# Which engine's queue issues the mixer's stores: SyncE's or ScalarE's

## The chip, the cores and the metric

The kernel runs on one core of a Trainium2 chip. The metric is the device time of one execution in microseconds, lower is better. An execution's time is a little longer than its span, the time from the first to the last instruction in the trace. TensorE (PE) does the matrix products, VectorE (DVE), ScalarE (ACT) and GpSimd (POOL) the element-wise work. SyncE (SP) computes nothing here and only issues DMAs. An engine runs its instructions in order, and when one of them waits for a semaphore, everything behind it on that engine waits too; this holds for the instruction that issues a DMA as for any other.

## What is computed

One layer of a hybrid encoder on 17 chunks of 128 tokens: chunk 0 holds 8 running streams of 16 new frames, chunks 1 to 16 hold one new stream of 2048 frames. All arithmetic is in f32.

```python
proj = jnp.einsum('bld,de->ble', x, w_in)              # 1024 -> u, v, z (1024 each), xbc 1536, dt 16
y_g  = gelu(u) * (W_s @ layer_norm(gelu(v)) + b_s)     # gMLP: a causal 128x128 product per head and chunk
xbc  = silu(causal_conv(xbc))                          # four taps over time
y    = ssd_scan(x, softplus(dt + bias), a, B, C, h0)   # Mamba-2: products inside a chunk, a state between chunks
y_s  = gated_rms_norm(y + d_skip * x, z, g)
x    = layer_norm(ALPHA * x + concat([y_g, y_s]) @ w_out)
x    = layer_norm(ALPHA * x + (relu(x @ w_ff1) ** 2) @ w_ff2)
```

## The kernel before, in words

**Phases.** The mixer (projection, convolution, scan, gMLP) runs until about 1066 us of the span; then come the product with w_out and the first norm, and after them the two products of the feed-forward part, which the change doesn't touch. An f32 product is made of three passes over split operands: `split` (L55, L56) casts a tile on ACT to its high part and subtracts on DVE for the low part.

**Blocks and units.** The mixer goes over the chunks in three blocks of 6, 6 and 5. In each block 18 units run in the order z0, x4, x5, x0, x1, z1, x2, x3, z2, z3, u0 to u3, v0 to v3. A unit multiplies the block's tokens by 256 columns of w_in. One group of 24 matmuls (8 slices of the contraction in 3 passes) fills one of four PSUM tiles (pool psA): of 128x384 in `fl_matmul` (L231) for x and u, of 128x256 in `tl_matmul` (L239) for z and v. Elementwise work empties the tile: for u and v `gelu2`, whose four steps alternate between ACT and DVE (L245 ACT, L246 DVE, L247 ACT, L248 DVE) and which reads PSUM until its last step; for z one ACT step (L275) and one on DVE (L276); for x two ACT steps (L301, L302), the convolution on DVE (L308), L313 on ACT and a product on DVE. PE may thus be ahead of that work by the tiles that are free, and no further.

**What goes through DRAM.** In block 0 the weights of a unit are loaded from w_in (L133), split, and both parts are kept in DRAM by L127 (2 MB a unit, 18 times); blocks 1 and 2 load them back by L117. The units' outputs go to DRAM too: u by L257, v by L266, z by L279, B and C by L328, x by L330 and by L334 (four DMAs of 32 partitions a unit). Between the units stand tasks: the scan of a chunk and group (`ssd`), which loads x, bt, bc, e and z (L418 to L427), and ends with a square on ACT (L505), a small root on POOL and a product on DVE (L507), stored by L508; and the gMLP of a chunk (`gmlp`), which loads v and u (L523, L525), multiplies on PE (L537) and then on POOL (L546), and stores by L547. The gMLP tasks of a block run in the first third of the next one, those of block 2 beside the product with w_out, whose weights are loaded by L631 and scaled by L636 (ACT) and L637 (DVE).

**The order.** The kernel is written in program order; a scheduler in the build sets the order on each engine, and the semaphores follow from it. Every DMA is issued by SP, and its landing counts on one of eight landing semaphores, taken in turn by all DMAs of the program: before a DMA is issued, its engine also waits for the landing of the one that took the same semaphore before.

```python
def gelu2(out, ps, n):
    t = ap.tile([P, 384], F32, name="gt", tag="gt", bufs=3)
    nc.scalar.activation(t[:, :n], ps, AF.Square)
    nc.vector.scalar_tensor_tensor(t[:, :n], t[:, :n], 1.0 / GC, ps, op0=ALU.add, op1=ALU.mult)
    nc.scalar.activation(t[:, :n], t[:, :n], AF.Tanh, scale=GK * GC)
    nc.vector.scalar_tensor_tensor(out, t[:, :n], 1.0, ps, op0=ALU.add, op1=ALU.mult)
```

The functions that the change touches, and what calls them:

Of the kernel before, what the change touches and what calls it, by code (L numbers as in the profile page):

```python
# [7 lines left out]
F32 = mybir.dt.float32  # L8
# [6 lines left out]
P = 128  # L15
# [75 lines left out]
def mixer_heads(ctx, tc, right, psA, A, O, dr, small, sp, ident, select, rsqrt, split, yg_d, ys_d):  # L91
    nc = tc.nc
# [31 lines left out]
    def keep_parts(u, w):  # L124
        n = 272 if u == "z0" else 256
        parts[u] = dr.tile([P, 2, KD, n], F32, name=f"w_{u}")
        nc.sync.dma_start(parts[u], w[:, :, :, :n].bitcast(F32))  # L127

    def load_w_half(w, u, q):
        n = 272 if u == "z0" else 256  # L130
# [119 lines left out]
    def unit_u(b, w, q):  # L250
        c0, n = BLOCKS[b]
        uo = ap.tile([P, 2, 6 * P], F32, name="uo", tag="ao")
        for f in range(2):
            for o, m in halves(n):
                ps = fl_matmul(w, f, o, m)
                gelu2(uo[:, f, o:o + m], ps[:, :m], m)
        nc.sync.dma_start(state[b]["u"][:, 2 * q:2 * q + 2, :], uo[:, :, :n * P])  # L257

    def unit_v(b, w, q):
        c0, n = BLOCKS[b]  # L260
        vo = ap.tile([P, 6, 256], F32, name="vo", tag="ao")
        for j in range(n):
            ps = tl_matmul(w, j, 256)
            gelu2(vo[:, j], ps[:, :256], 256)
            nc.vector.bn_stats(state[b]["vst"][:, j, q], vo[:, j])
        nc.sync.dma_start(state[b]["v"][:, :, q * 256:(q + 1) * 256].rearrange("c p f -> p c f"), vo[:, :n])  # L266

    def unit_z(b, w, q):
        c0, n = BLOCKS[b]
        nn = 272 if q == 0 else 256  # L270
        zo = ap.tile([P, 6, 256], F32, name="zo", tag="ao")
        for j in range(n):
            ps = tl_matmul(w, j, nn)
            t = ap.tile([P, 384], F32, name="zt", tag="gt", bufs=3)
            nc.scalar.activation(t[:, :256], ps[:, :256], AF.Tanh, scale=0.5)  # L275
            nc.vector.scalar_tensor_tensor(zo[:, j], t[:, :256], 1.0, ps[:, :256], op0=ALU.add, op1=ALU.mult)  # L276
            if q == 0:
                nc.vector.tensor_add(state[b]["dt"][:, j], ps[:, 256:272], dtb)
        nc.sync.dma_start(state[b]["z"][:, :, q * 256:(q + 1) * 256].rearrange("c p f -> p c f"), zo[:, :n])  # L279

    def unit_x(b, w, q):
        c0, n = BLOCKS[b]
        nd = 1 if c0 == 0 else 0
        npr = (n - nd) * P
        fl_out = ap.tile([P, 2, 6 * P], F32, name="fo", tag="ao") if q >= 4 else None
        tl_out = ap.tile([P, 6, 256], F32, name="to", tag="ao") if q < 5 else None
        for f in range(2):
            ft = 2 * q + f
            raw = ap.tile([P, 3 + 6 * P], F32, name="raw", tag="raw", bufs=1)
            acc = ap.tile([P, 6 * P], F32, name="acc", tag="acc")  # L290
            nc.gpsimd.tensor_copy(raw[:, :3], carry[:, ft])
            if nd:
                rawd = ap.tile([P, NS, 3 + DS], F32, name="rawd", tag="rawd", bufs=1)
                nc.gpsimd.tensor_copy(rawd[:, :, :3], cst_in[:, ft])
            for o, m in halves(n):
                ps = fl_matmul(w, f, o, m)
                s = 0
                if nd and o == 0:
                    s = P
                    nc.scalar.copy(rawd[:, :, 3:], ps[:, :P].rearrange("p (s t) -> p s t", s=NS))  # L300
                nc.scalar.copy(raw[:, 3 + o + s - nd * P:3 + o + m - nd * P], ps[:, s:m])  # L301
                nc.scalar.activation(acc[:, o:o + m], ps[:, :m], AF.Identity, bias=cb[:, ft:ft + 1], scale=cw[:, ft, 3:4])  # L302
            for k in range(3):
                if nd:
                    ad = acc[:, :P].rearrange("p (s t) -> p s t", s=NS)
                    nc.vector.scalar_tensor_tensor(ad, rawd[:, :, k:k + DS], cw[:, ft, k:k + 1], ad, op0=ALU.mult, op1=ALU.add)
                aa = acc[:, nd * P:n * P]
                nc.vector.scalar_tensor_tensor(aa, raw[:, k:k + npr], cw[:, ft, k:k + 1], aa, op0=ALU.mult, op1=ALU.add)  # L308
            nc.gpsimd.tensor_copy(carry[:, ft], raw[:, npr:npr + 3])
            if nd:  # L310
                nc.gpsimd.tensor_copy(cst_out[:, ft], rawd[:, :, DS:])
            t = ap.tile([P, 6 * P], F32, name="ct", tag="ct", bufs=1)
            nc.scalar.activation(t[:, :n * P], acc[:, :n * P], AF.Tanh)  # L313
            dst = fl_out[:, f, :n * P] if q >= 4 else acc[:, :n * P]
            nc.vector.scalar_tensor_tensor(dst, t[:, :n * P], 1.0, acc[:, :n * P], op0=ALU.add, op1=ALU.mult)
            if q < 4:

                nc.vector.transpose(tl_out.rearrange("p c (k f) -> p (c k) f", f=64)[:, :4 * n, 32 * f:32 * f + 32],
                                    dst.rearrange("p (k i) -> p k i", i=32))
            if q == 4:  # L320
                for j0 in range(0, n, 3):
                    m = min(3, n - j0)
                    pt = psB.tile([P, 4, P], F32, name="pt", tag="b")
                    for j in range(m):
                        nc.tensor.transpose(pt[:, j], dst[:, (j0 + j) * P:(j0 + j + 1) * P], ident)
                    nc.scalar.copy(tl_out[:, j0:j0 + m, f * P:(f + 1) * P], pt[:, :m])
        if q >= 4:
            nc.sync.dma_start(state[b]["bc"][:, :, q - 4, :], fl_out[:, :, :n * P])  # L328
        if q == 4:
            nc.sync.dma_start(state[b]["xs"][:, :, q * 256:(q + 1) * 256].rearrange("c p f -> p c f"), tl_out[:, :n])  # L330
        if q < 4:
            xs = state[b]["xs"].rearrange("c (m i) f -> i (c m) f", i=32)
            for c in range(4):
                nc.sync.dma_start(xs[:, :, q * 256 + c * 64:q * 256 + c * 64 + 64],  # L334
                                  tl_out[32 * c:32 * c + 32, :n].rearrange("p c (k f) -> p (c k) f", f=64))


# [71 lines left out]
    def ssd(b, j, g):  # L409
# [95 lines left out]
        nc.scalar.activation(t, y, AF.Square, accum_out=ss)  # L505
        rsqrt(ss, ss, 1.0 / 512, 4 * EPS)
        nc.vector.tensor_scalar(y, y, ss, None, op0=ALU.mult)  # L507
        nc.sync.dma_start(ys_d[c0 + j][:, g * 512:(g + 1) * 512], y)  # L508


    def gmlp(b, j):
# [7 lines left out]
        for q in range(2):  # L519
            hq = slice(4 * q, 4 * q + 4)  # L520
            fq = slice(512 * q, 512 * q + 512)
            v = half("v")
            nc.sync.dma_start(v, s["v"][j, :, fq])  # L523
            u = half("ug").rearrange("p (k t) -> p k t", k=4)
            nc.sync.dma_start(u, s["u"][:, hq, j * P:(j + 1) * P])  # L525
            nc.vector.tensor_scalar(v, v, mv[:, 0:1], rs, op0=ALU.subtract, op1=ALU.mult)
            wm = wt[:, hq]
            if dec:
                wm = half("wt8").rearrange("p (k t) -> p k t", k=4)
                nc.vector.memset(wm, 0.0)  # L530
                for r in range(NS):
                    nc.sync.dma_start(wm[r * DS:(r + 1) * DS, :, r * DS:(r + 1) * DS], A["gmlp_wsT"][:DS, hq, :DS])
                select(wm, [[0, 4], [1, P]], 0, -1)
            ps = psB.tile([P, 4, P], F32, name="sg", tag="b")
            o = fp.tile([P, 4, P], F32, name="og", tag="og", bufs=2)
            for i in range(4):
                nc.tensor.matmul(ps[:, i], v[:, i * P:(i + 1) * P], wm[:, i], start=True, stop=True)  # L537
            for i in range(4):
                h = 4 * q + i
                if dec:  # L540
                    k = cst[:, h, :DS].unsqueeze(1).to_broadcast([P, NS, DS])
                    i0, oo = ps[:, i].rearrange("p (s t) -> p s t", s=NS), o[:, i].rearrange("p (s t) -> p s t", s=NS)
                else:
                    k, i0, oo = cst[:, h], ps[:, i], o[:, i]
                nc.vector.scalar_tensor_tensor(oo, i0, lgh[:, h:h + 1], k, op0=ALU.mult, op1=ALU.add)
            nc.gpsimd.tensor_mul(u, u, o)  # L546
            nc.sync.dma_start(yg_d[c0 + j][:, hq, :], u)  # L547
            if dec:
                for i, nm in enumerate(("gmlp_ln_g", "gmlp_ln_b")):
                    k = half("lk")  # L550
                    nc.sync.dma_start(k, row(nm)[:, fq].to_broadcast([P, 512]))
                    (nc.vector.tensor_mul, nc.vector.tensor_add)[i](v, v, k)
                nc.sync.dma_start(O["v_sample"][:, fq], v)
# [608 lines left out]
```

## Time and profile before

| | us |
|---|---|
| median of 3 runs | 2829.03 (2822.79 to 2832.81) |
| the profiled execution | 2822.72 |
| its span | 2821.0 |
| PE busy | 2753.9 (98%) |
| DVE busy | 1816.1 (64%) |
| ACT busy | 1096.0 (39%) |
| POOL busy | 395.1 (14%) |

The profiled execution is 6.3 us, 0.2%, under the median. Busy times leave out the issuing of DMAs and all waiting. In the rows further down an instruction that issues a DMA has the engine's name with a q (SPq), `out<-in` are tile names, `x3` is how many instructions a row joins, and `[1.93 <-DVE vo L248]` says that the engine stood idle for 1.93 us ahead of it until DVE's instruction at L248 on tile vo had ended. Idle time of PE is what counts where it is 98% busy; idle time of the others counts only where it ends in one of PE's.

### The profile page before, as it was taken

The numbers are of one execution on the slowest core, as the hardware profiler recorded it, in microseconds if no ns is written. First come the engines' busy times: TensorE is split into PE (matmuls) and PEld (weight loads), VectorE is DVE, ScalarE is ACT, GpSimd is POOL, SyncE is SP. The second block draws the span as 40 slices with busy tenths as digits, with TensorE's granted clock in tenths as the row PEclk, the third lists the DMA queues.
The fourth block names the chain that finished last, engine by engine and source line by source line (L and its number), as shares of the span: only waits on it lengthen the run. The fifth ranks groups of instructions, "written<-read, shape, count | busy, mean of one in ns | idle before, by whom it ended". The sixth has DMA issues, their size and how long they took to land.

```text
span 2821.0 us, 42133 instructions
## 1 busy us (share of the span) xinstructions
PE 2753.9 (98%) x15814; PEld 2525.6 (90%) x15814; DVE 1816.1 (64%) x2836; ACT 1096.0 (39%) x2024; POOL 395.1 (14%) x547
## 2 busy tenths in 40 slices
PE   9999999999999998999989999999999999999998
PEld 8988899999999997887879999999999888888886
DVE  6766667645585457665558667667775356644887
ACT  5445423323333333100115556556665323333343
POOL 2214223323233312000100000000000000000022
PEclk9999999999999999999999999999999999999999
DMA  9897888766697768888579858667877468855764
GB/s 316 257 297 250 281 288 272 228 221 217 218 305 220 244 218 302 279 260 273 159 217 342 292 214 286 222 223 259 276 233 259 152 233 300 299 173 190 272 206 171
DMA packets 492316, 699.83 MB, mean 248 GB/s; under 512 B 74560, under 2 KB 379088, under 8 KB 485584
## 3 DMA queue, kind: packets, MB, share of 16 engines
q1 hardware_dynamic: 492112, 697.14, 74.8%
q8 instruction: 124, 2.03, 0.3%
q14 instruction: 80, 0.66, 0.1%
HBM read 474.04 MB, written 223.00 MB: 247 GB/s over the span
## 4 chain that ended last, share of the span: by engine, by line
PE 77%; DMA 12%; DVE 6%; issue 1%; ACT 1%; POOL 1%; SPq 1%; DVEq 0%; ACTq 0%; POOLq 0%
PE pf L858 22%; PE pf L1075 22%; PE psfl L231 13%; PE pstl L239 10%; PE po L683 4%; PE yd L446 2%; DMA w1p<-in_w_ff 2%; DMA w1s<-w1p 2%; PE pf L1040 2%; DMA v<-v 1%; DMA xv<-xtt 1%; PE st L483 1%; DMA v<-vo 1%; DMA e<-at 1%; PE yo L489 1%
## 5 line engine op out<-in xcount | busy, mean ns | idle before, releaser
L858 PE MATMUL pf<-xt,w 128*128 128x384 f32 (+1 forms) x4032 | 671.8, 329 | 14.6 <-ACT w L55 11.4
L858 PEld LDWEIGHTS pf<-xt,w 128*128 128x128 f32 x4032 | 669.2, 189 | 17.4 <-ACT w L55 12.3
L1075 PE MATMUL pf<-w,ht 128*128 128x512 f32 x2688 | 618.2, 389 | 0.0
L1075 PEld LDWEIGHTS pf<-w,ht 128*128 128x128 f32 x2688 | 504.6, 188 | 104.6
L231 PE MATMUL psfl<-xw,w 128*128 128x384 f32 (+1 forms) x2880 | 494.9, 330 | 0.0
L231 PEld LDWEIGHTS psfl<-xw,w 128*128 128x128 f32 x2880 | 475.5, 188 | 9.0 <-issue 8.6
L239 PE MATMUL pstl<-w,xw 128*128 128x256 f32 (+1 forms) x3264 | 411.0, 286 | 8.4 <-ACT w L55 6.5
L239 PEld LDWEIGHTS pstl<-w,xw 128*128 128x128 f32 x3264 | 396.4, 190 | 21.0 <-issue 11.8
L683 PE MATMUL po<-wout,mx 128*128 128x512 f32 x1632 | 379.5, 394 | 12.0 <-ACT mx L55 8.1
L683 PEld LDWEIGHTS po<-wout,mx 128*128 128x128 f32 x1632 | 309.2, 190 | 79.1 <-ACT mx L55 8.8
L56 DVE TENSOR_TENSOR ht<-hr,ht 128x1536 fp32r<-128x1536 f32 (+1 forms) x84 | 132.3, 1577 | 128.0 <-ACT ht L55 126.5
L76 POOL TENSOR_SCALAR frs<-fmv 128x1 f32<-128x1 f32 x17 | 8.9, 524 | 1291.6 <-DVE fmv L996 1291.0
L55 ACT CAST ht<-hr 128x1536 fp32r<-128x1536 f32 (+1 forms) x84 | 112.2, 1337 | 194.7 <-PE pf L1075 142.0
L56 DVE TENSOR_TENSOR w<-w1s,w 128x512 fp32r<-128x512 f32 x192 | 132.0, 691 | 41.0 <-ACT w L55 36.0
L55 ACT CAST w<-w1s 128x512 fp32r<-128x512 f32 x192 | 118.3, 619 | 64.1 <-PE pf L858 57.0
L308 DVE SCALAR_TENSOR_TENSOR acc<-raw,cw,acc 128x640 f32<-128x640 f32 (+1 forms) x108 | 111.4, 1031 | 14.1 <-ACT acc L302 12.7
L56 DVE TENSOR_TENSOR w<-w2r,w 128x512 fp32r<-128x512 f32 x144 | 93.8, 686 | 36.8 <-ACT w L55 36.6
L55 ACT CAST w<-w2r 128x512 fp32r<-128x512 f32 x144 | 83.3, 618 | 87.3 <-PE pf L1075 56.9
L438 ACT ACTIVATE e<-e,nacum 128x128 f32<-128x128 f32 x272 | 83.6, 389 | 66.8 <-POOL e L69 66.7
L55 ACT CAST w<-w1r 128x512 fp32r<-128x512 f32 x96 | 59.4, 618 | 98.6 <-PE pf L858 95.3
L247 ACT ACTIVATE gt<-gt 128x256 f32<-128x256 f32 (+1 forms) x116 | 52.3, 451 | 95.9 <-DVE gt L246 95.9
L849 ACT ACTIVATE hc<-hc 128x384 f32<-128x384 f32 (+3 forms) x144 | 87.1, 608 | 1.8
(214 smaller groups left out, 2875.4 us busy)
## 6 DMA issues: line engine op xcount, KB each, us to landing
w1s<-w1s SPq DMA_DIRECT2D x48, 1024.0 KB, 6.7
hr<-hv SPq DMA_DIRECT2D x56, 768.0 KB, 6.1
w2r<-in_w_ff SPq DMA_DIRECT2D x112, 256.0 KB, 5.6
w<-w_x SPq DMA_DIRECT2D x12, 2048.0 KB, 10.5
w1r<-in_w_ff SPq DMA_DIRECT2D x48, 512.0 KB, 6.7
hv<-hs SPq DMA_DIRECT2D x32, 768.0 KB, 5.2
ws<-in_w_in SPq DMA_DIRECT2D x34, 512.0 KB, 7.7
e<-at SPq DMA_DIRECT2D x34, 512.0 KB, 6.7
```

What stands on the lines that cost most here:

```text
L55: nc.scalar.copy(hi, src)
L56: nc.vector.tensor_sub(lo, src, hi.bitcast(F32))
L231: nc.tensor.matmul(ps[:, :n], w[:, a, k, f * P:(f + 1) * P], xw[:, b, k, o:o + n], start=(q, i, k) == KORDER[0], stop=(q, i, k) == KORDER[-1])
L239: nc.tensor.matmul(ps[:, :n], xw[:, a, k, j * P:(j + 1) * P], w[:, b, k, :n], start=(q, i, k) == KORDER[0], stop=(q, i, k) == KORDER[-1])
L308: nc.vector.scalar_tensor_tensor(aa, raw[:, k:k + npr], cw[:, ft, k:k + 1], aa, op0=ALU.mult, op1=ALU.add)
L438: nc.scalar.activation(e[:, h], e[:, h], AF.Exp, bias=s["nacum"][:, i:i + 1])
L446: nc.tensor.matmul(yd[:, h * HD:(h + 1) * HD], e[:, h], xdt[:, h * HD:(h + 1) * HD], start=True, stop=True)
L683: nc.tensor.matmul(acc[c][d], m[c][k // 4][:, a, k % 4], W[q][:, w, i, d * 512:(d + 1) * 512], start=k == 0 and (a, w) == (0, 0), stop=k = ...
L849: nc.scalar.activation(t, t, AF.Square)
L858: nc.tensor.matmul(o, W[i][:, u, k], X[i][:, v, k, :n], start=q + k == 0 and not more, stop=q == 2 and k == 3, skip_group_check=True)
L1040: nc.tensor.matmul(ps[d], h[:, u, k, f], w[d][:, v], start=k + f + q == 0, stop=(k, f, q) == (n - 1, 1, 2))
L1075: nc.tensor.matmul(acc[l], h[:, u, m, j * P:(j + 1) * P], w[m][:, v], start=kg + q + m == 0, stop=(kg, q, m) == (3, 2, 3))
```

## The change

All nine stores that the mixer's units and tasks make are issued from ACT instead of SP; the loads and a few stores of results (L480, L494, L553, the convolution's carry) stay on SP. That is 179 DMAs: L127 18, L257 12, L266 12, L279 12, L328 6, L330 3, L334 48, L508 34, L547 34. SP's program goes from 1279 rows to 1115, ACT's from 1613 to 1770. From the second group of the product with w_out on, the order of both programs is the same.

```diff
@@ -124,7 +124,7 @@
-        nc.sync.dma_start(parts[u], w[:, :, :, :n].bitcast(F32))
+        nc.scalar.dma_start(parts[u], w[:, :, :, :n].bitcast(F32))
@@ -254,7 +254,7 @@
-        nc.sync.dma_start(state[b]["u"][:, 2 * q:2 * q + 2, :], uo[:, :, :n * P])
+        nc.scalar.dma_start(state[b]["u"][:, 2 * q:2 * q + 2, :], uo[:, :, :n * P])
@@ -263,7 +263,7 @@
-        nc.sync.dma_start(state[b]["v"][:, :, q * 256:(q + 1) * 256].rearrange("c p f -> p c f"), vo[:, :n])
+        nc.scalar.dma_start(state[b]["v"][:, :, q * 256:(q + 1) * 256].rearrange("c p f -> p c f"), vo[:, :n])
@@ -276,7 +276,7 @@
-        nc.sync.dma_start(state[b]["z"][:, :, q * 256:(q + 1) * 256].rearrange("c p f -> p c f"), zo[:, :n])
+        nc.scalar.dma_start(state[b]["z"][:, :, q * 256:(q + 1) * 256].rearrange("c p f -> p c f"), zo[:, :n])
@@ -325,13 +325,13 @@
-            nc.sync.dma_start(state[b]["bc"][:, :, q - 4, :], fl_out[:, :, :n * P])
+            nc.scalar.dma_start(state[b]["bc"][:, :, q - 4, :], fl_out[:, :, :n * P])
-            nc.sync.dma_start(state[b]["xs"][:, :, q * 256:(q + 1) * 256].rearrange("c p f -> p c f"), tl_out[:, :n])
+            nc.scalar.dma_start(state[b]["xs"][:, :, q * 256:(q + 1) * 256].rearrange("c p f -> p c f"), tl_out[:, :n])
-                nc.sync.dma_start(xs[:, :, q * 256 + c * 64:q * 256 + c * 64 + 64],
+                nc.scalar.dma_start(xs[:, :, q * 256 + c * 64:q * 256 + c * 64 + 64],
@@ -505,7 +505,7 @@
-        nc.sync.dma_start(ys_d[c0 + j][:, g * 512:(g + 1) * 512], y)
+        nc.scalar.dma_start(ys_d[c0 + j][:, g * 512:(g + 1) * 512], y)
@@ -544,7 +544,7 @@
-            nc.sync.dma_start(yg_d[c0 + j][:, hq, :], u)
+            nc.scalar.dma_start(yg_d[c0 + j][:, hq, :], u)

```

The scheduler places each store in ACT's order. Three places follow. In the first, the end of block 0's unit v2 (the tiles `w_v_3834` and `v_264` in DRAM are the kept weights of v3 and the block's v), SP had this before:

```order
L418 DMA xs<-xs_266 128x512
L127 DMA w_v_3834<-w 2048x1x256
L266 DMA v_264<-vo 128x6x256
L139 DMA xs_in<-in_xT 128x1024
L508 DMA ys_97<-xs 128x512
```

and ACT has this in the changed program:

```order
L438 ACTIVATE e<-e,nacum_272 128x128 x8
L127 DMA w_v_3834<-w 2048x1x256
L266 DMA v_264<-vo 128x6x256
L247 ACTIVATE gt<-gt 128x256
L245 ACTIVATE gt<-pstl 128x256
```

The store of the kept weights and behind it that of a finished v unit now stand between two steps of ACT's own work, ahead of the gelu steps of the next chunk.

The second place is ACT in the x units of block 1, where the gMLP tasks of block 0 run (`raw`, `acc` and `ct` are the convolution's tiles, `ug` the gMLP's result). Before:

```order
L313 ACTIVATE ct<-acc 128x768
L301 COPY raw<-psfl 128x384
L302 ACTIVATE acc<-psfl,cb,cw 128x384
L301 COPY raw<-psfl 128x384
L302 ACTIVATE acc<-psfl,cb,cw 128x384
L313 ACTIVATE ct<-acc 128x768
```

and in the changed program:

```order
L313 ACTIVATE ct<-acc 128x768
L301 COPY raw<-psfl 128x384
L302 ACTIVATE acc<-psfl,cb,cw 128x384
L301 COPY raw<-psfl 128x384
L302 ACTIVATE acc<-psfl,cb,cw 128x384
L547 DMA yg_80<-ug 128x512 x2
L313 ACTIVATE ct<-acc 128x768
```

Two stores of the gMLP's result, each of which waits for POOL's product, now stand ahead of L313.

The third place is ACT beside the first group of the product with w_out. Before, eight steps of L636 follow one another:

```order
L55 CAST mx<-myt 128x512 x2
L55 CAST wout<-wos 128x1024 x2
L55 CAST mx<-myt 128x512 x2
L636 ACTIVATE wout<-wos,ng 128x1024 x8
L55 CAST mx<-mxs 128x512 x2
```

and in the changed program:

```order
L547 DMA yg_90<-ug 128x512 x2
L636 ACTIVATE wout<-wos,ng 128x1024 x2
L547 DMA yg_91<-ug 128x512
L636 ACTIVATE wout<-wos,ng 128x1024
L547 DMA yg_91<-ug 128x512
L547 DMA yg_92<-ug 128x512
L636 ACTIVATE wout<-wos,ng 128x1024
L547 DMA yg_92<-ug 128x512
L636 ACTIVATE wout<-wos,ng 128x1024 x2
```

The stores of the last chunks' gMLP results now stand among the steps of L636.

## Rows read from the trace of the kernel before

**Rows 1.** The page's first part: busy time, share of the span, instructions.
```profile
PE 2753.9 (98%) x15814; PEld 2525.6 (90%) x15814; DVE 1816.1 (64%) x2836; ACT 1096.0 (39%) x2024; POOL 395.1 (14%) x547
```
**Rows 2.** Windows: stretch, length, busy us per engine, PEclk, DMA share, GB/s.
```profile
0.00:383.00 383.00, 368.48 (x2420) 347.58 (x2420) 257.09 (x431) 172.76 (x371) 108.89 (x194) 1.00 0.87 282
...
420.00:757.00 337.00, 334.63 (x2300) 322.60 (x2299) 204.39 (x343) 115.78 (x286) 106.82 (x128) 1.00 0.71 229
...
1065.00:1128.00 63.00, 53.81 (x257) 43.54 (x256) 49.76 (x91) 19.36 (x25) 19.95 (x18) 0.95 0.95 322
```
**Rows 3.** Waits of PE, 0 to 1128 us: total us, times, longest.
```profile
PE sg L537 <- DVE v L526: 5.2, 3, 3.3
PE yo L475 <- DMA h<-in_state_ssm: 3.8, 3, 2.2
...
PE pc L429 <- DMA bc<-bc: 2.2, 2, 1.2
...
PE pstl L239 <- DVE vo L248: 1.9, 1, 1.9
PE yd L446 <- POOL xdt L441: 1.8, 1, 1.8
```
**Rows 4.** PE's timeline: start, length us, what, count (one row of two stretches).
```profile
372.05 10.99 PE L239 MATMUL pstl<-w,xw 128*128 128x256 f32 x88
...
452.74 16.97 PE L231 MATMUL psfl<-xw,w 128*128 128x384 f32 x96
```
**Rows 5.** Waits of SP's queue, 0 to 1128 us: total us, times, longest.
```profile
SPq L508 <- DVE xs L507: 86.7, 20, 8.2
SPq L418 <- DMA ys<-xs: 57.1, 28, 4.8
```
**Rows 6.** Instructions of L508, L334, L279: ns of one issue, min/median/max.
```profile
L508 SPq DMA_DIRECT2D ys<-xs x34: 319/320/1357, 198.9 to 1031.3; - x34
...
L334 SPq DMA_DIRECT2D xs<-to x48: 318/747/3372, 94.5 to 904.3; - x48
...
L279 SPq DMA_DIRECT2D z<-zo x12: 371/1268/3622, 30.7 to 932.5; - x12
```
**Rows 7.** SP's timeline at the end of block 0 (v1 to v3).
```profile
326.89 3.12 SPq L266 DMA_DIRECT2D v<-vo  x1
...
353.38 0.53 SPq L127 DMA_DIRECT2D w_v<-w  x1
354.00 3.60 SPq L266 DMA_DIRECT2D v<-vo  x1
...
372.82 10.25 SPq L139 DMA_DIRECT2D xs_in<-in_xT  x2
```
**Rows 8.** ACT's timeline at the end of block 0.
```profile
357.64 0.42 ACT L247 ACTIVATE gt<-gt 128x256 f32<-128x256 f32 x1 [3.02 <-DVE gt L246]
...
383.08 0.42 ACT L247 ACTIVATE gt<-gt 128x256 f32<-128x256 f32 x1 [5.11 <-DVE gt L246]
```
**Rows 9.** Timelines of ACT and POOL in block 1's x units.
```profile
462.91 0.85 ACT L313 ACTIVATE ct<-acc 128x768 f32<-128x768 f32 x1 [8.74 <-DVE acc L308]
...
480.03 0.85 ACT L313 ACTIVATE ct<-acc 128x768 f32<-128x768 f32 x1 [6.58 <-DVE acc L308]
...
460.01 1.99 POOL L546 TENSOR_TENSOR ug<-ug,og 128x512 f32<-128x512 f32 x1 [2.52 <-DVE og L545]
...
475.22 3.90 POOL L546 TENSOR_TENSOR ug<-ug,og 128x512 f32<-128x512 f32 x2 [1.74 <-DVE og L545]
```
**Rows 10.** Timelines of POOL, ACT and PE beside the first w_out group.
```profile
1120.92 1.44 POOL L546 TENSOR_TENSOR ug<-ug,og 128x512 f32<-128x512 f32 x1 [4.20 <-DVE og L545]
1123.83 2.20 POOL L546 TENSOR_TENSOR ug<-ug,og 128x512 f32<-128x512 f32 x1 [1.46 <-DMA wos<-in_w_out]
...
1122.26 1.15 ACT L636 ACTIVATE wout<-wos,ng 128x1024 fp32r<-128x1024 f32 x1 [1.53 <-DMA wos<-in_w_out]
...
1124.94 5.32 PE L683 MATMUL po<-wout,mx 128*128 128x512 f32 x22 [1.55 <-DVE wout L637]
```

## The prediction, made before the changed kernel was run

> **What bounds the kernel now.** I read the busy times first: PE is busy for 98% of the span, ACT for 39% [rows 1]. Next come the windows, because the change touches only the mixer and the first product with w_out, which fill the first 1128 us; there PE is busy for 368.48 of 383 us in block 0 and for 334.63 of 337 us in the x, z, u and v units of block 1, and only 53.81 of 63 us at the start of the w_out product [rows 2]. So nothing that the change does to ACT or SP counts until PE waits for it. Then I read what PE waits for [rows 3]. Four of its waits end with data that a load brought: sg behind the scaled v 5.2, h 3.8, bc 2.2 and xdt (the loaded xs times dt) 1.8 us, 13.0 us together. A quicker queue of loads can give back this much and hardly more. One other wait matters below: 1.9 us for DVE's last gelu step (vo), at the border of blocks 0 and 1. SP itself waits a lot, 86.7 us at L508 for DVE alone [rows 5], but SP computes nothing; its waits cost only what arrives in the 13.0 us.
>
> Last I measured how far ACT may fall behind before PE notices. PE needs 10.99 us for 88 matmuls of 128x256, so 24 x 10.99 / 88 = 3.0 us for a group that fills one PSUM tile, and 24 x 16.97 / 96 = 4.2 us for one of 128x384 [rows 4]. There are four tiles. With one being emptied, three are cover: about 9.0 us in z and v units, 12.7 us in x and u units, provided that ACT and DVE were not already behind.
>
> **Part by part: what leaves SP.** 179 issues and their waits leave it, 86.7 us of waits at L508 being the largest entry. The loads behind them can go out earlier, but not all do: L418 waits 57.1 us for the landing of ys<-xs [rows 5], that is, its tile comes free only when the store has landed, and which engine issued the store changes nothing in that. Bounds of the gain: nothing, and the whole 13.0 us. I take a quarter, 3.3 us, since the largest wait of a load names a landed store and not a held queue.
>
> **What ACT gets as work.** No row shows a DMA issued by ACT in this kernel. The nearest rows are SP's: 0.320 us the median at L508, 0.747 at L334, 1.268 at L279 [rows 6]. For these 94 issues that is 34 x 0.320 + 48 x 0.747 + 12 x 1.268 = 62 us; the other 85 at 0.32 to 1.27 us are 27 to 108 us. So ACT gets 89 to 170 us in the first 1128 us, at the least nothing if it issues for free, and never a gain. That is up to 15% more of its time, on top of 45% in block 0 (172.76 of 383) and 34% in block 1 (115.78 of 337) [rows 2]. Spread in pieces of about 1 us under a cover of 9.0 to 12.7 us, it costs nothing. If the cover is gone (ACT and DVE already behind), each piece counts in full.
>
> **What ACT gets as waits.** A store waits for the last producer of its tile (DVE's L507, L248, L276; POOL's L546), for a landing semaphore, and for room in the queue. Behind the waiting store stand ACT's next gelu, tanh or cast steps; for these wait DVE, then the PSUM tile, then PE.
>
> - Steady units. The order in ACT puts L508 one or a few steps behind L505, and two small POOL steps and L507 lie between. I count 1 to 2 us a time, an estimate from lengths of steps like these; well inside 9.0 us. Cost 0.
> - Block 1's x units. Two stores of ug stand ahead of L313. POOL's products end at 460.01 + 1.99 = 462.00 and 475.22 + 3.90 = 479.12 us; L313 itself starts only at 462.91 and 480.03, having waited 8.74 and 6.58 us for DVE [rows 9]. The new wait lies inside the old one: cost 0. The work that covers it is DVE's convolution; were DVE earlier, up to the 3.90 us of the POOL pair would show.
> - End of block 0. Behind the 2 MB store of kept weights the next issue takes long: L266 took 3.12 us at 326.89, and 3.60 us at 354.00, right after L127 at 353.38 [rows 7]. In the changed order both stand on ACT, ahead of the next gelu steps. ACT is not early there: it waits for DVE between two steps of one gelu, 3.02 us at 357.64 [rows 8]. So the cover is thin, and part of the hold lies in that wait. Between nothing and 3.12 + 3.60 = 6.7 us I take half, 3.4 us.
> - Border of blocks 0 and 1. L266 of unit v2 stands near the loads of x for block 1. The pair of loads behind it held SP for 10.25 us [rows 7], because of tiles and landings not yet free. If that store holds ACT as long, 10.25 us meet a cover of 9.0 us, of which nothing is left at the border: ACT already waits 5.11 us for DVE at 383.08 [rows 8], and PE 1.9 us for DVE's step [rows 3]. Bounds: nothing (the hold lies inside the 5.11 us and more), and 10.25. I take 2.0 us, near the wait that PE has there now.
> - Start of the w_out product. Of the last stores, one stands ahead of the sixth L636 and one ahead of the seventh. The seventh started at 1122.26; POOL's last product ends at 1123.83 + 2.20 = 1126.03 [rows 10], so it would start 3.8 us later. PE waits here for DVE's step behind it (1.55 us at 1124.94 [rows 10]), so no cover is left. In the other direction, the loads of w_out and v no longer stand behind L547 on SP, which brings L636 and POOL's chain forward. Bounds: nothing and 3.8; I take half, 1.9 us.
>
> **The sum.** 3.4 + 2.0 + 1.9 - 3.3 = +4.0 us. Against the profiled execution, 2822.72 + 4.0 = 2826.7 us. That execution lies 6.3 us under the median of 2829.03, and the price adds to either, so the median becomes 2833.0 us. About 0.3%, 8.5 us, is what a measurement of this kernel can tell from no change: the forecast is inside it.
>
> **Rivals.**
>
> A, faster: the loads come early. If every wait of PE that a load ends goes, and ACT's holds stay covered everywhere, the time is 2829.0 - 13.0 = 2816.0 us. For it: SP waits 86.7 us at L508 with loads queued behind. Against it: L418's 57.1 us name the landing of a store [rows 5], the DMA engines are 71 to 87% busy in blocks 0 and 1 and 95% at the w_out product [rows 2], and 5.2 of the 13.0 us lie at the gMLP's v, which a store must write first. The Trainium skill, page "Perfetto Trace Analysis", section on DMA optimizations, advises what this change does: one engine for input DMAs and another for output DMAs. By that advice the time would be A's.
>
> B, slower: ACT is held for longer than the PSUM tiles cover. Its place is the end of block 0, units v1 to v3 and the border, and the same hold at the sixth and seventh L636. It decides from the point where a hold is longer than three groups, 9.0 us, or where ACT enters it already behind. Its price is 3.12 + 3.60 + 10.25 + 3.8 = 20.8 us, hence 2849.8 us. For it: ACT is at 45% in block 0, in which the 18 stores of 2 MB fall, and it waits for DVE already. Against it: each hold would have to reach PE whole.
>
> C, no change: the two queues stay coupled. The eight landing semaphores are shared by all DMAs, so a load on SP may still wait for the landing of a store on ACT and a store for a load's, and PE's waits stay where they are: 2829.0 us. Apart from that, the Trainium skill, page "DMA: Bandwidth & Descriptors", section "Issuing engines are not separate DMA queues", says that DMAs of all issuers run on the same 16 engines and that a second issuer saves only the time of issuing. By this the loads would gain little, which is C's side; the 3.12 and 3.60 us of issuing behind a full store [rows 7] show that here the saved part is not always small.
>
> **How the numbers follow.** Chances: the forecast 0.45, A 0.15, B 0.27, C 0.13. The forecast's own range is 2822 to 2841 us (its terms at a half up or down). Low end of the range: A's 2816. High end: B's 2849.8 plus the 3.90 us of the block 1 units, were their cover gone, about 2854. Some 0.07 lies below and 0.11 above. Faster by over 0.3% (below 2820.5) is most of A: 0.13. Slower by over 0.3% (above 2837.5) is B and the upper end of the forecast, 0.27 + 0.07 = 0.34. Within 0.3%: C, the rest of the forecast and of A, 0.53.
>
> **What would show it.** In the profile after: SP's waits at L508 are gone, and L418's for ys<-xs have stayed. PE's waits for load-ended tiles go from 13.0 to about 10 us; if they fall to 3 or less and nothing comes in, A is right. At the end of block 0 ACT issues L266 with 3 us or more behind L127, and PE's waits for vo grow from 1.9 to some 7 us; if they grow by 15 or more, B is right. Beside the w_out product ACT's L636 is held until POOL's L546 ends, and PE's wait for wout grows by about 2 us. L313 in block 1 starts no later against the PE groups than before. The forecast is wrong if ACT's issues take much longer than 0.3 to 1.3 us each, since then the steady units pay too, or if the order of PE's tasks, which the scheduler also moved, lets PE wait in a place where it did not wait before.

## The result

The changed kernel is slower: 2843.84 us in the median of 13 runs (2834.71 to 2851.01) against 2824.44 us for the kernel before in the same sessions. The ratio, estimated from all runs and not from the two medians (whose quotient is 1.0069), is 1.0058, with a 95% interval of 1.0046 to 1.0071, or +16 us on the 2829.03 us that the prediction started from. That is inside the range of 2816 to 2854 us, but only because the range reaches to rival B's price: it is above the forecast's own 2822 to 2841 us, four times the forecast of +4.0 us, and nearer to rival B (+20.8 us). Rivals A (faster) and C (no change) did not come.

The changed kernel's profiled execution took 2834.71 us, the lowest of its 13; its span is 2833.0 us, 12.0 us more than before. So the traces below show 12 of the some 16 us. The first lines are from the page of the changed kernel: busy times, then DMA queues (q10 is ACT's).

```profile
PE 2759.2 (97%) x15814; PEld 2527.8 (89%) x15814; DVE 1811.8 (64%) x2836; ACT 1093.0 (39%) x2024; POOL 396.7 (14%) x547
...
q1 hardware_dynamic: 387616, 599.09, 63.9%
q10 hardware_dynamic: 104496, 98.05, 10.0%
```

The change does what it says: 98 MB go through a second queue. PE runs the same 15814 matmuls and is busy for 5.3 us longer than in [rows 1] (2759.2 - 2753.9); the other 6.7 of the 12.0 us are idle time. The mean granted clock of the two profiled executions is the same, 0.991, but it falls to 0.50 in other places. Up to the second group of the w_out product it stands at 0.50 for 27 us in all in the changed kernel and for 14 us in the kernel before, which costs PE some 7 us more; behind that it is the other way round, 17 against 27 us. In the changed kernel a stall of PE began ahead of each fall.

Next, what PE waits for in the changed kernel, 0 to 1140 us: total us, times, longest.

```profile
PE yd L446 <- DVE e L439: 7.8, 7, 2.1
...
PE yd L446 <- POOL xdt L441: 5.9, 5, 1.9
PE sg L537 <- DVE v L526: 4.7, 2, 3.7
PE yo L475 <- DMA h<-in_state_ssm: 2.7, 2, 2.1
PE po L683 <- DVE wout L637: 2.5, 2, 1.6
...
PE psfl L231 <- DVE zo L276: 1.6, 1, 1.6
PE po L683 <- ACT wout L636: 1.5, 1, 1.5
```

The four load-ended waits of [rows 3], 13.0 us, are now xdt 5.9, v 4.7, h 2.7 and bc 0: 13.3 us. Nothing was gained there. What grew are the waits of the scan's product yd, for e (after DVE) and xdt (after a load of xs). The wait for vo is gone. SP's queue (same view) shows what became of its waits:

```profile
SPq L418 <- DMA ys<-xs: 196.2, 25, 12.3
```

The waits of [rows 5] at L508 (86.7 us) left SP and came back at the load of xs, which needs the landing of the same store: 57.1 us have become 196.2.

**Where the time goes.** I took the start of the first matmul of each unit in both traces; the table gives how much later the changed kernel is (us), over five stretches. The last column is the second half of the first w_out group, from its 97th matmul to the second group's first. Unit names are those of the order of units, with the block ahead: 0x5-0x0 is from the start of x5 to that of x0 in block 0. "Rest 1, 2" is what else blocks 1 and 2 lose until the w_out product.

```
kernel (which stores ACT issues)   0x5-0x0  0x0-1z0  1z1-1z2  rest 1, 2  w_out 1st-2nd group   ratio
changed (all nine)                   3.7      8.7      8.0      -5.9          3.3              1.0058
all but L127                         0.0     15.3      7.9      -4.4          5.1              1.0039
all but L508                         3.5     17.3      8.7       0.5          5.0              1.0076
all but L334                         3.6      6.7      0.3       0.9          4.9              1.0011
all but L547                         2.9     13.7      7.1      -5.4          0.4              1.0050
all but L127, L334                   0.0      8.7      0.0       4.8          4.1              1.0014
only L127                            0.0      5.2      0.0       6.7          1.8              1.0018
only L334                            0.0      9.5      0.0       1.4          0.8              1.0030
only L508                            0.0      2.4      0.0       1.8          2.0              0.9993
only L508, L547                      0.0     -2.4      0.0       1.0          1.4              0.9996
none, four more copies on ACT        0.0     -0.1      0.0      -1.0          2.5              0.9992
L127 on POOL                         0.0     -1.1      0.0       4.5          0.3              0.9975
all nine on POOL                     0.0     -2.1      1.5       8.7          2.2              1.0040
```

The first and third columns are sharp: a loss is there or it is not. The second is spread, since the scheduler also places the scans anew in most of these kernels. The ratios come from several runs, the columns from one execution each, and one execution can stray: behind the columns, from the second w_out group on, where the change touches nothing, these traces differ from the one before by -5.9 to +8.3 us.

### The profile page after: what moved, and what is told of

Read it like the earlier page. It is cut to its first block, busy times and chain, and to the rows that moved or that the text cites. A ratio compares the mean times of both kernels' runs of the same rounds, so it can differ in the third digit from the quotient of the medians.

```text
span 2833.0 us, 42155 instructions
## 1 busy us (share of the span) xinstructions
PE 2759.2 (97%) x15814; PEld 2527.8 (89%) x15814; DVE 1811.8 (64%) x2836; ACT 1093.0 (39%) x2024; POOL 396.7 (14%) x547
## 4 chain that ended last, share of the span: by engine, by line
PE 68%; DMA 15%; DVE 9%; ACT 3%; issue 2%; ACTq 1%; POOL 1%; SPq 1%; DVEq 0%; POOLq 0%
PE pf L1075 22%; PE pf L858 22%; PE psfl L231 8%; PE pstl L239 8%; PE po L683 3%; DMA w1p<-in_w_ff 2%; PE yd L446 2%; DMA w1s<-w1p 2%; PE pf L1040 2%; DMA e<-at 1%; DVE acc L308 1%; DVE w L56 1%; PE st L483 1%; ACTq L334 1%; DMA xs<-to 1%
## 5 line engine op out<-in xcount | busy, mean ns | idle before, releaser
L858 PE MATMUL pf<-xt,w 128*128 128x384 f32 (+1 forms) x4032 | 669.8, 328 | 14.9 <-ACT w L55 12.0
L231 PEld LDWEIGHTS psfl<-xw,w 128*128 128x128 f32 x2880 | 476.8, 188 | 12.8 <-issue 10.2
L55 ACT CAST mx<-mxs 128x512 fp32r<-128x512 f32 x34 | 20.1, 620 | 162.9 <-DMA mxs<-yg 98.4
```

The lines of the kernel that those rows point to most:

```text
L55: nc.scalar.copy(hi, src)
L231: nc.tensor.matmul(ps[:, :n], w[:, a, k, f * P:(f + 1) * P], xw[:, b, k, o:o + n], start=(q, i, k) == KORDER[0], stop=(q, i, k) == KORDER[-1])
L858: nc.tensor.matmul(o, W[i][:, u, k], X[i][:, v, k, :n], start=q + k == 0 and not more, stop=q == 2 and k == 3, skip_group_check=True)
```

## The experiments

Theory H: ACT, held while it issues or waits for a store, makes DVE's steps and the scans late. Theory D: the stores of ys land later, and so do the loads that wait for them. Theory O: only the order that the scheduler made of it is worse.

**L127 back on SP.**

```diff
+        nc.sync.dma_start(parts[u], w[:, :, :, :n].bitcast(F32))      # L127, the rest as changed
```

> The changed kernel with L127, the 2 MB stores of the kept weights, back on SP. In the changed kernel (1.0058 of before, about +16 us) the stores behind L127 held ACT for 3.56 (L328), 6.23 and 4.56 us (L266). Theory H (ACT is held while it issues a store behind a full one, and DVE's steps for gelu and scan come late): these three fall below 1 us each, block 0 gives back most of its 12 us, and the ratio to before is 1.001 to 1.003. Theory D (the stores of ys wait in ACT's order, land later, and the scans' loads of xs with them): L127 is no part of it, the ratio stays at 1.004 to 1.006. Theory O (the scheduler put PE's tasks in a worse order, the queues matter little): anything, the ratio follows the order and no single hold.

Measured: 1.0039 (1.0022 to 1.0055), between what H and D expected. The loss between x5 and x0 of block 0 is gone, and there the chain can be read line by line. ACT's timeline in the changed kernel at the start of block 0, and then with L127 back on SP (start, us, what):

```profile
29.76 0.58 ACTq L127 DMA_DIRECT2D w_x<-w  x1
30.39 6.01 ACTq L279 DMA_DIRECT2D z<-zo  x1
36.45 0.28 ACT L348 ACTIVATE u<-na 128x96 f32<-128x96 f32 x1 [6.53 <-issue]
```

```profile
29.77 0.40 ACTq L279 DMA_DIRECT2D z<-zo  x1
32.17 0.28 ACT L348 ACTIVATE u<-na 128x96 f32<-128x96 f32 x1 [2.73 <-DVE na L346]
```

PE's timeline and windows (length, busy us of PE, PEld, DVE, ACT, POOL, then PEclk, DMA share, GB/s) of the changed kernel:

```profile
47.41 0.36 PE L370 MATMUL pa<-da,tri 128*128 128x16 f32 x2 [1.87 <-DVE da L364]
...
47.00:48.86 1.86, 1.45 (x12) 1.36 (x12) 1.82 (x7) 1.86 (x4) 0.35 (x1) 1.00 1.09 386
48.87:52.28 3.41, 3.41 (x13) 2.98 (x13) 3.41 (x7) 1.71 (x5) 1.50 (x2) 0.50 0.53 184
```

Behind the 2 MB store the next issue holds ACT for 6.01 us instead of 0.40. The step behind it (L348, for the decays) runs 4.3 us later, DVE's chain to da as much, and PE stalls for 1.87 us. Then the clock is granted at 0.50 of full speed for 3.4 us, which costs 1.7 us, where the kernel with L127 on SP shows 1.00. So the loss of 3.7 us is half stall, half clock. It appears in exactly the four kernels with L127 and the unit stores both on ACT.

In the same way the two L266 behind L127 hold ACT at the end of block 0. ACT, DVE, PE and a window of the changed kernel:

```profile
323.38 6.23 ACTq L266 DMA_DIRECT2D v<-vo  x1
329.66 0.39 ACT L245 ACTIVATE gt<-pstl 128x256 f32<-128x256 f32 x1 [8.67 <-issue]
...
352.38 4.56 ACTq L266 DMA_DIRECT2D v<-vo  x1
...
330.07 0.42 DVE L246 SCALAR_TENSOR_TENSOR gt<-gt,pstl 128x256 f32<-128x256 f32 x1 [4.30 <-ACT gt L245]
...
334.41 1.20 DVE L439 TENSOR_TENSOR e<-e,pc 128x1024 f32<-128x1024 f32 x1
...
335.67 3.68 PE L446 MATMUL yd<-xdt,e 128*128 128x64 f32 x16 [2.09 <-DVE e L439]
...
335.59:342.41 6.82, 6.74 (x25) 5.71 (x26) 6.20 (x15) 2.44 (x7) 1.19 (x3) 0.50 0.96 273
```

These are 6.23 and 4.56 us where SP's were 3.12 and 3.60 [rows 7]. PE does not wait for a PSUM tile of the v unit. It waits for e of a scan, whose DVE step (L439) stands behind the late gelu steps: DVE had stood idle for 4.30 us for ACT's L245. Then PE runs at 0.50, the lower level of its clock (1.2 GHz), for 6.8 us: 16 products of yd take 3.68 us instead of 1.89 at full clock (the kernel before at 511.72 us). But without L127 on ACT the rest of block 0 lost more (15.3 against 8.7 us), with other scans in other places; so these holds don't account for block 0 as a whole. Most of what is lost there is the clock: from x0 to the end of block 0 it stands at 0.50 for 10 us in the changed kernel and for 24 us with L127 back on SP, while the kernel before shows 1.00 [rows 2].

**L508 back on SP.**

```diff
+        nc.sync.dma_start(ys_d[c0 + j][:, g * 512:(g + 1) * 512], y)  # L508, the rest as changed
```

> The changed kernel with L508, the 34 stores of ys, back on SP. Theory D: SP's wait of L418 for ys<-xs falls from 196.2 us to about the 57.1 of before, PE's waits at yd for xdt from 5.9 to about 2 us, and the ratio to before goes from 1.0058 to about 1.002. Theory H: the holds of 3.56, 6.23 and 4.56 us in block 0 and of 3.1 us at L334 stay, ratio 1.004 to 1.006.

Measured: 1.0076 (1.0055 to 1.0097), slower still. L418's wait fell as D said, to 54.9 us, but PE's waits for xdt did not (7.3 us), and it did not help. With L508 alone on ACT (below) the same wait is 163.3 us, and that kernel loses nothing. So D is refuted: the wait comes with L508 and is not what costs.

**L334 back on SP.**

```diff
+                nc.sync.dma_start(xs[:, :, q * 256 + c * 64:q * 256 + c * 64 + 64],   # L334, the rest as changed
```

> The changed kernel with L334, the 48 small stores of xs, back on SP. Theory H in block 1: four issues of L334 held ACT for 3.13 us at 515.71 us, z's PSUM tiles came free late and PE lost 5.5 us between units x2 and x3. Without them that loss goes: 12 us of delay at the start of block 1 and no more than that after it, ratio about 1.003 to 1.004. Theory D: no change in the ratio, 1.005 to 1.006.

Measured: 1.0011 (0.9999 to 1.0022), a larger gain than H expected: of the single stores, L334 gives back the most. The place in block 1 in the changed kernel, ACT, then PE, then a window:

```profile
496.24 3.14 ACTq L334 DMA_DIRECT2D xs<-to  x4
...
515.71 3.13 ACTq L334 DMA_DIRECT2D xs<-to  x4
518.89 1.32 ACT L275 ACTIVATE zt<-pstl 128x256 f32<-128x256 f32 x4 [5.15 <-PE pc L429]
...
519.78 4.99 PE L231 MATMUL psfl<-xw,w 128*128 128x384 f32 x27 [1.63 <-DVE zo L276]
526.66 3.64 PE L446 MATMUL yd<-xdt,e 128*128 128x64 f32 x16 [1.89 <-POOL xdt L441]
...
526.74:533.55 6.81, 6.81 (x21) 4.80 (x21) 1.38 (x2) 0.00 (x0) 5.00 (x5) 0.50 1.08 365
```

ACT waits for DVE's transpose, then issues four stores in 3.13 us; four finished PSUM tiles of z1 wait meanwhile, and PE finds no free one (1.63 us). The stores are late, so the scan's load of xs is late, xdt too (1.89 us), and the clock is at 0.50 for 6.8 us behind it. Two stalls of 3.5 us together cost 8.0.

**Only L127 on ACT.**

```diff
-        nc.sync.dma_start(parts[u], w[:, :, :, :n].bitcast(F32))
+        nc.scalar.dma_start(parts[u], w[:, :, :, :n].bitcast(F32))    # L127, the rest as before
```

> The kernel before with only L127 moved to ACT. The stores and loads that stood behind it on SP (3.12 to 3.79 us each) issue at once; on ACT nothing that issues stands behind it. Theory H: ACT is held for no longer than one issue (about 0.5 us, 18 times), so no loss, and perhaps a small gain: ratio 0.998 to 1.000. Theory O: the order of PE moves here too, and the ratio may be anything from 0.997 to 1.005.

Measured: 1.0018 (1.0005 to 1.0032), no gain but a small loss, though no ACT hold is left and the order on PE, as its trace shows it, differs from before by one matmul. The cause of the 5.2 us in block 0 is on SP: its wait between 295 and 335 us, the landing times of L127 in the kernel before and in this one, POOL and PE there:

```profile
SPq L423 <- DMA w_v<-w: 11.3, 1, 11.3
```

```profile
DMA to landing us min/median/max: 7.6/9.2/14.9
...
DMA to landing us min/median/max: 8.9/15.9/19.1
```

```profile
330.14 1.04 POOL L441 TENSOR_TENSOR xdt<-xs,dt 128x512 f32<-128x512 f32 x1 [1.85 <-DMA xs<-xs]
...
331.24 3.67 PE L446 MATMUL yd<-xdt,e 128*128 128x64 f32 x16 [4.98 <-POOL xdt L441]
```

On SP the 2 MB stores landed after 9.2 us in the median (14.9 at most); on ACT after 15.9 (19.1). A small load on SP that has the same landing semaphore waits 11.3 us for one of them, all loads stand behind it, xdt comes late, and PE loses 4.98 us and then runs at half clock. This is the coupling of rival C, with a price instead of none. The other 6.7 us arise in block 2, where yd waits for e (5.8 us, 2.0 before); what makes e late there I did not find.

**Only L334 on ACT, and L127 and L334 both back.**

```diff
-                nc.sync.dma_start(xs[:, :, q * 256 + c * 64:q * 256 + c * 64 + 64],
+                nc.scalar.dma_start(xs[:, :, q * 256 + c * 64:q * 256 + c * 64 + 64],   # L334, the rest as before
```

> The kernel before with only L334, the 48 small stores of xs, moved to ACT. With L334 back on SP the changed kernel fell from 1.0058 to 1.0011 of before, and PE's loss between units x2 and x3 of block 1 (8.0 us) was gone. Theory H: L334 alone is enough for it; ACT waits for DVE's transpose and issues four stores in about 3.1 us, PE loses 7 to 9 us at that place, and the ratio is 1.002 to 1.004. Theory O (it was the order that came with it): no loss at that place, ratio 0.999 to 1.001.

Measured: 1.0030 (1.0016 to 1.0045), the size that H gave, but not at its place: between z1 and z2 of block 1 it lost nothing. ACT's and PE's timelines of this kernel there, and ACT's in block 0:

```profile
510.61 3.12 ACTq L334 DMA_DIRECT2D xs<-to  x4
513.77 0.66 ACT L275 ACTIVATE zt<-pstl 128x256 f32<-128x256 f32 x2 [5.14 <-issue]
...
500.66 17.18 PE L239 MATMUL pstl<-w,xw 128*128 128x256 f32 x144
...
112.32 7.15 ACTq L334 DMA_DIRECT2D xs<-to  x4
119.58 0.94 ACT L275 ACTIVATE zt<-pstl 128x256 f32<-128x256 f32 x3 [9.23 <-DMA xs<-to]
```

The same hold of 5.14 us begins 8 us after PE entered z1, and the PSUM tiles cover it; in the changed kernel it began 14 us after (z1 at 500.11, the last step ahead of the hold at 513.7), since the steps ahead of it were late already: x1's first L313 ran 3.7 us ahead of z1's start in the kernel before (486.09) and 2.0 us ahead of it here (498.70), but 3.7 us behind it in the changed kernel (503.80). So a hold costs by where it falls, not by its length alone. In block 0 the four issues take 7.15 us, and ACT stands for 9.23 us, just over the cover of 9.0 us. PE stalls there, though not at a PSUM tile: it waits 1.78 us for the next scan's xdt, and the clock falls behind that. The kernel with L127 and L334 both back has a stall of 1.52 us at the same product, so L334 is not all that makes it.

> The changed kernel with both L127 and L334 back on SP. If the two costs are separate, what each gave back adds: 1.0058 less 0.0019 (L127) less 0.0047 (L334) is 0.999, so 0.998 to 1.000: no hold of ACT over 1 us in block 0 and none at x2 and x3 in block 1. If L127's cost in block 0 is a matter of order alone, block 0 keeps a loss of 5 us or more and the ratio stays at 1.001 to 1.003.

Measured: 1.0014 (0.9999 to 1.0028). Both sharp losses are gone, as expected, but block 0 keeps 8.7 us. The costs of L127 and L334 are not additive, and what remains in block 0 has no single cause that I could name.

**L547 back on SP.**

```diff
+            nc.sync.dma_start(yg_d[c0 + j][:, hq, :], u)               # L547, the rest as changed
```

> The changed kernel with L547, the 34 stores of the gMLP's results, back on SP. Theory H at the w_out product: the two stores ahead of the sixth and seventh L636 cost PE 3.3 us between the first and second group there (5 us in the runs with L127, L508 or L334 back); that goes to 0 to 2 us. The rest stays: ratio 1.003 to 1.006.

Measured: 1.0050 (1.0033 to 1.0067). In the last column of the table the loss falls from 3.3 to 0.4 us, as H said. ACT there in the changed kernel:

```profile
1131.83 5.99 ACTq L547 DMA_DIRECT2D yg<-ug  x2
1137.87 1.15 ACT L636 ACTIVATE wout<-wos,ng 128x1024 fp32r<-128x1024 f32 x1 [8.53 <-DMA yg<-ug]
...
1139.07 1.19 PE L683 MATMUL po<-wout,mx 128*128 128x512 f32 x4 [1.52 <-ACT wout L636]
```

ACT is held for 8.53 us ahead of L636, 5.99 us of it in two issues. The loss in block 1 stays (7.1 us), so it does not need L547.

**Only L508; L508 and L547; four more copies on ACT.**

```diff
+        nc.scalar.dma_start(ys_d[c0 + j][:, g * 512:(g + 1) * 512], y)   # only L508 on ACT; with L547 in the second kernel
```

> The kernel before with only L508, the stores of ys, moved to ACT. With L508 back on SP the changed kernel became slower (1.0058 to 1.0076), so on ACT these stores may help: SP loses its largest wait (86.7 us at L508 for DVE) and loads go out earlier. Theory G (this part of the change is a gain): the ratio is 0.997 to 0.999, PE's load-ended waits of 13.0 us fall. Theory D (late landing): ratio 1.001 to 1.003. No effect by itself: 0.999 to 1.001.

> The kernel before with only L508 and L547 moved to ACT, the 68 stores that gave SP its waits for DVE and POOL. L508 alone gave 0.9993. If freeing SP of these waits is worth something where ACT gets no long hold: ratio 0.996 to 0.999. If L547's holds in block 1 and beside L636 cost what it gives: 0.999 to 1.002.

Measured: 0.9993 (0.9978 to 1.0008) and 0.9996 (0.9982 to 1.0011): no difference. With L508 alone the order on PE, DVE and POOL is that of the kernel before, row for row. So this is the queue alone. But SP was not freed by it: the waits at L508 came back at L418.

```profile
SPq L418 <- DMA ys<-xs: 163.3, 27, 12.3
```

Waits that move from one of SP's instructions to another neither gain nor cost anything that can be measured. The next kernel is the one before with four copies added on ACT:

```diff
-            xs = state[b]["xs"].rearrange("c (m i) f -> i (c m) f", i=32)
+            xs = state[b]["xs"].rearrange("c (m i) f -> i (c m) f", i=32); [nc.scalar.copy(t, tl_out[:, :3].rearrange("p c f -> p (c f)")) for c in range(4)]
```

> The kernel before, all stores on SP, with four copies of 128x768 on ACT behind the transposes of each unit x0 to x3 (they read the tile that L334 stores and write one that is free; extra work without use). Each is about 0.8 us, so four take as long as L334's four issues on ACT, 3.1 us, and wait for the same step of DVE. L334 alone on ACT gave 1.0030. Theory H (what costs is ACT being held): the same loss, ratio 1.002 to 1.004. If the cost lay in the DMAs being on a second queue (later landing, shared landing semaphores): 0.999 to 1.001.

Measured: 0.9992 (0.9977 to 1.0007), against H as I had put it. But ACT's timeline shows that the scheduler put other steps between the copies:

```profile
498.74 0.84 ACT L332 COPY ct<-to 128x768 f32<-128x768 f32 x1 [2.02 <-DVE to L318]
499.48 0.38 ACT L275 ACTIVATE zt<-pstl 128x256 f32<-128x256 f32 x1
499.75 2.56 ACT L332 COPY ct<-to 128x768 f32<-128x768 f32 x3
```

It shows that 3.4 us more of work on ACT per x unit cost nothing. It doesn't test a hold as long as L334's (5.1 us in block 1, 9.2 in block 0).

**POOL as the issuer.**

```diff
-        nc.sync.dma_start(parts[u], w[:, :, :, :n].bitcast(F32))
+        nc.gpsimd.dma_start(parts[u], w[:, :, :, :n].bitcast(F32))    # L127 alone; all nine in the second kernel
```

> The kernel before with only L127 moved, to POOL's queue. With L127 alone on ACT (1.0018) it landed after 15.9 us in the median (9.2 on SP), and SP stood for 11.3 us at L423 until one of these had landed, since all DMAs of SP and ACT take the same landing semaphores in turn; POOL's DMAs take others. If that coupling was the cost: SP's waits for w_v and w_u landings are gone and the ratio is 0.998 to 1.001. If slower sharing of the DMA engines was, or POOL pays for issuing 2 MB: 1.002 or more.

Measured: 0.9975 (0.9960 to 0.9990): faster than both kernels. SP's timeline in this kernel right behind the fourth and third to last L127 (281.80 and 300.73 us, on POOL), and at the v store of [rows 7]:

```profile
281.89 0.46 SPq L257 DMA_DIRECT2D u<-uo  x1
...
301.41 0.33 SPq L257 DMA_DIRECT2D u<-uo  x1
...
325.01 0.43 SPq L266 DMA_DIRECT2D v<-vo  x1
```

SP issues in 0.33 to 0.46 us where right behind L127 it took 3.12 [rows 7], and it no longer waits for the landing of a w store. These stores land late on POOL's queue too, after 13.0 us in the median, so their late landing alone is not what costs. POOL pays 1.11 to 1.17 us an issue for most of them. Where the gain of 0.25%, 7 us, comes from is not shown: the one profiled execution (2828.35 us) is among the slowest of its 12.

> All nine stores of the change issued from POOL instead of ACT. POOL is busy for 14% of the span, and only the scans' selects and products and the gMLP's product stand behind a held store. Theory H (ACT's place was the trouble): the loss of 0.58% goes, ratio 0.998 to 1.001. If any engine with work of its own is the wrong place, or issuing costs POOL more than 1 us each: 1.004 or more, with PE waiting for xdt and e.

Measured: 1.0040 (1.0025 to 1.0055). Blocks 0 and 1 lose almost nothing, but block 2 loses 9 us. So moving the 18 large stores to POOL gains a little, and moving all nine loses.

## Why the prediction was right or wrong

**Right.** PE bounds the mixer, and ACT has time to spare for work (3.4 us more per x unit costs nothing). The mechanism of the loss, where it could be shown, is rival B's: a held ACT. That L418 would keep waiting for the landing of ys<-xs was right, though the wait grew. The place beside the w_out product was right too, and its loss of 3.3 us lies between the 1.9 taken and the bound of 3.8; but the hold there was the issuing of two stores (5.99 us) more than the wait for POOL, and PE's waits for wout grew by 0.5 us (3.5 to 4.0) and not by 2. That the time lies in the stated range is owed to the range's width: the sum itself came out at a quarter of the loss.

**The step that failed: L334 was priced as work, not as a wait.** In the part on ACT's work it went in with 0.747 us an issue, in pieces of about 1 us under the cover; it is missing from the list of waits. But four of them follow one another, with a wait for DVE ahead: ACT was held for 5.1 us in block 1 and up to 10.2 us in block 0. The median hid it; [rows 6] has the maximum of 3372 ns beside it. Without it the ratio falls from 1.0058 to 1.0011. The steady units and block 1 were put at 0 and cost 8.0 us in one place; L313, which was to start no later against PE's groups there, ran 3.7 us behind the start of z1 where it had run 3.7 us ahead of it.

**Mis-sized: the hold behind 2 MB.** Taken from SP as 3.12 and 3.60 us, it was 6.23 and 4.56 on ACT. And I had looked at two of its places only: in block 0 the next store behind an L127 takes 3.56 to 7.04 us to issue in eight places, 42 us in all. Most of that is covered (behind the longest, L257 at 253.03 us, the next wait of PE is 1.07 us); the one of 6.01 us (L279), at the start of block 0, cost 3.7 us. At the border of the blocks, where I took 2.0 us, L266 was issued in 0.38 us, and PE has no wait for vo left there.

**The cover was measured in the wrong coin.** I counted PSUM tiles of the units, 9.0 us. PE mostly stalled earlier, at the scan's products, which stand in its order among the units and wait for e and xdt: 7.8 + 5.9 us, where the kernel before has 1.8 for xdt [rows 3] and 2.0 for e:

```profile
PE yd L446 <- DVE e L439: 2.0, 2, 1.7
```

**The gain of 3.3 us did not come**: 13.0 us of load-ended waits became 13.3. And **the clock was missing from the sum**: of the 17.8 us that the changed kernel's trace has lost when the second w_out group starts, some 7 are PE at 0.50 of its clock, behind the new stalls.

**Open.** Why the rest of block 0 loses between -2 and 17 us over these kernels; the order on PE changes with most edits, and only the kernels with L508 alone and, but for one matmul, with L127 alone keep it. Why L508 on SP makes the changed kernel slower. From the second w_out group on, the changed kernel's trace wins back 5.9 us: one wait of PE for mx is shorter by 3.2 us (6.1 before, 2.9 after), and the clock stands at 0.50 for 10 us less; I can't tell that from chance.

## What to carry to other kernels

A store moved to a computing engine brings along its wait, its landing semaphore and whatever the queue holds ahead of it; price it as the longest hold in its place (several in a row, or one behind a large store), not as a median issue. Ask which instruction stands behind it and what in TensorE's order first needs that: it may be another task's product and not the accumulator. Large stores are better issued from an engine where nothing urgent stands behind them; here that was GpSimd, for 18 of 179 stores and 0.25% of the time.

## What the runs showed of the hardware

A 2 MB store on a queue of its own landed later, not sooner: after 15.9 us in the median on ACT's and 13.0 us on POOL's, against 9.2 us in the queue of the loads. Four issues of 32-partition stores took 3.1 to 3.9 us in block 1 and 7.1 to 8.9 us in block 0 on ACT; on POOL an issue of L334 took 0.68 to 0.77 us throughout.

And a short stall of PE can cost more than itself. In the changed kernel, stalls of 1.9 to 2.1 us ahead of small products (128x16 or 128x64) were followed by 3.4 to 6.8 us at 0.50 of the clock, in the windows shown above, which costs 1.7 to 3.4 us. It does not always happen. In the kernel before, PE stalled for 1.83 us ahead of yd at 254.74 us and for 1.69 us ahead of yd at 895.48 us; the windows behind the two, of the kernel before:

```profile
256.00:260.00 4.00, 4.00 (x22) 3.04 (x22) 0.79 (x2) 1.80 (x7) 4.00 (x4) 1.00 1.08 378
...
897.00:901.00 4.00, 4.00 (x12) 2.45 (x12) 3.14 (x6) 0.74 (x1) 3.44 (x3) 0.50 1.05 342
```

The first kept 1.00, the second fell to 0.50. What decides between them is not shown by these runs.
